# Reciprocal roots of the norms: a power operation on GpSimd in place of an integer guess and three Newton steps on VectorE

## The chip, the cores and the metric

The kernel runs on one core of a Trainium2 chip. The core has a matrix engine (TensorE, PE in the profile), a vector engine (VectorE, DVE), a scalar engine (ScalarE, ACT), a general engine (GpSimd, POOL) and a queue engine (SyncE, SP) that here only issues DMA transfers. Each engine works through its own list of instructions in order and waits on semaphores for results of the others. The metric is the device time of one execution in microseconds (us).

## The reference

One layer of an encoder over 1024 rows of 1024 features, in float32. Three blocks are added to the running rows, and a last norm closes the layer:

```python
x = x + 0.5 * swiglu_half_step(x, ffn1_norm, ffn1_w_in, ffn1_w_out)
x = x + hybrid_mixer(x, ...)      # attention heads and recurrent heads side by side
x = x + 0.5 * swiglu_half_step(x, ffn2_norm, ffn2_w_in, ffn2_w_out)
x = rms_norm(x, final_norm)

def rms_norm(x, gain):
    return x * lax.rsqrt(jnp.mean(x * x, axis=-1, keepdims=True) + 1e-6) * gain
```

The norm appears in many places: before each of the three blocks and at the end over a row of 1024 features, for each attention query and key head and each recurrent output head over 128 features, and over the 512 features of the attention output. In each of them the sum of squares of a row is turned into one factor, the reciprocal root of (sum / width + 1e-6). How that factor is computed is all that the change touches.

## The kernel before

Rows are handled in eight tiles of 128 rows, one row per partition, so a norm of a tile needs one factor per partition. `rstd(ss, n, width, tag)` (line 72) gets n sums of squares per partition and gives n factors. It is called 43 times:

- `pair1` (line 1224) normalizes the eight input tiles in pairs: the first two tiles by a call each with n = 1, the other three pairs by one call each with n = 2. ScalarE squares and sums the tile (line 1236), and one VectorE operation multiplies by factor and gain (line 1240).
- `row_rstd` and `norm_rows` (lines 118 and 129) do the same for the eight tiles ahead of the mixer (`done1`, names `n1`), the eight ahead of the second feed-forward block (`to_ffn`, names `n2`) and the eight of the output (`done2`, names `fin`), each with n = 1. The multiplication is line 132; where a row is worked in two halves, line 126 first adds the two sums.
- `head_norm` (line 825) has n = 8: four calls for the recurrent heads (`rec`), four for queries (`aq`), two for keys (`ak`). It squares on ScalarE, sums on VectorE (line 831), multiplies by the factor on VectorE (line 833) and by the gain on GpSimd (line 836).
- `attn_scale` (line 1064) has n = 2 and is called four times (`ao`): a matmul with a column of ones sums the squares, and the factor enters where the projection's result leaves PSUM (line 1079).

Inside, `rstd` works on VectorE alone. Line 83 scales the sums and adds the small constant, lines 84 and 85 make a first guess with integer operations on the bits of the number, and three Newton steps follow. A step is two operations when n = 1 (lines 89 and 95) and three otherwise (lines 93, 94, 95). So a call has 9 VectorE operations when n = 1 and 12 otherwise, each on at most 128 x 8 numbers and each needing the one before it.

The matmuls are arranged in stages. In `ffn_up` the normalized tiles are transposed on TensorE (line 183), split into two parts (lines 191 and 192; the difference on VectorE or GpSimd), and multiplied with weights that are loaded by SyncE's queue (line 255) and split in the same way (lines 104 and 105). `plain` (line 285) has the first matmuls (line 295), `product` the later ones (line 311); sums of blocks for a Strassen scheme are formed on VectorE (lines 237 to 240) and GpSimd (lines 272 to 275). `ffn_down` (line 443) multiplies with the second weight (line 515), adds to the rows (lines 542 and 581), and calls `done` for a finished tile. After the first feed-forward block, `follow1` transposes the normalized tile (line 148) for the mixer, whose first matmuls are line 168. In `mixer_in` the recurrent heads run with raised priority and projections fill in between; `attention` softmaxes (GpSimd multiplies half of the probabilities, line 985), projects (line 1032) and sends the rows to the second block through DRAM (lines 1085 and 1091, issued from GpSimd's queue).

The order of instructions on each engine isn't written by hand. The program is laid out by a planner (`schedule_with_timeline_sim=True`, line 1374) that plays the instructions through on estimated durations and, at each moment, gives a free engine the ready instruction of the highest priority; the source order and the marked high-priority stretches set the priorities. The result is a fixed list per engine. Tiles of one pool tag share a few buffers, so a load into a buffer also waits until the last reader of its earlier content is done; the input tiles and the raw weights of `ffn_up` share seven buffers.

Of the kernel before, what the change touches and what calls it, by code (L numbers as in the profile page):

```python
# [12 lines left out]
F32 = mybir.dt.float32  # L13
F32R = mybir.dt.float32r
I32 = mybir.dt.int32
U8 = mybir.dt.uint8
AF = mybir.ActivationFunctionType
ALU = mybir.AluOpType
# [3 lines left out]
P = 128  # L22
# [10 lines left out]
NREC = 4  # L33
NCH = T // P
EPS = 1e-6
RS_SCALE = 2.0 ** -28
RS_MAGIC = 0x5F3759DF - (1 << 23) - (1 << 31)
WHOLE = (slice(0, D),)
HALVES = (slice(0, D // 2), slice(D // 2, D))
LEVELS = (1, 2, 4, 8, 16, 32, 64)  # L40
# [5 lines left out]
class Trunk:  # L46
    def __init__(self, ctx, tc, io):
        self.tc, self.nc, self.io = tc, tc.nc, io
        nc = self.nc
        pool = lambda name, **kw: ctx.enter_context(tc.tile_pool(name=name, **kw))  # L50
        self.const = pool("const", bufs=1)
        self.gpool = pool("gains", bufs=1)
        self.stat = pool("stat", bufs=4)
        self.dpool = pool("scratch", bufs=1, space=bass.MemoryType.DRAM)
        self.ident = self.const.tile([P, P], F32, name="ident")
        pool("align", bufs=1, side="right").tile([P, 40], F32, name="align")
        make_identity(nc, self.ident)
        self.banks = {}

    def open_psum(self, ctx, prefix, **spec):  # L60
# [11 lines left out]
    def rstd(self, ss, n, width, tag):  # L72

        nc = self.nc
        work = self.stat.tile([P, 9, n], F32, name=f"rs_{tag}", tag=f"rs{n}")  # L80
        parts = iter(work[:, i, :] for i in range(9))
        v, t, w = next(parts), next(parts).bitcast(I32), next(parts)
        nc.vector.tensor_scalar(v, ss, RS_SCALE / width, RS_SCALE * EPS, ALU.mult, ALU.add)
        nc.vector.tensor_single_scalar(t, v.bitcast(I32), 1, op=ALU.logical_shift_right)
        nc.vector.tensor_scalar(w.bitcast(I32), t, -1, RS_MAGIC, ALU.mult, ALU.add)
        for c in (0.75, 3.0 * 2.0 ** -4, 3.0 * 2.0 ** -10):
            q, y = next(parts), next(parts)
            if n == 1:
                nc.vector.scalar_tensor_tensor(
                    out=q, in0=w, scalar=v, in1=w, op0=ALU.mult, op1=ALU.mult  # L90
                )
            else:
                nc.vector.tensor_mul(q, w, w)
                nc.vector.tensor_mul(q, q, v)
            nc.vector.scalar_tensor_tensor(
                out=y, in0=q, scalar=-c, in1=w, op0=ALU.add, op1=ALU.mult
            )
            w = y
        return w

    def split(self, hl, src, lo_engine=None):
# [1276 lines left out]
```

## Time and profile before

| | |
|---|---|
| median of 3 runs | 2008.72 us (2003.79 to 2009.0) |
| profiled execution, its own time | 2008.14 us |
| span of its instructions | 2006.0 us |
| mean granted TensorE clock | 0.991 |
| TensorE matmul busy | 1944.5 us (97%) |
| TensorE weight load busy | 1665.6 us (83%) |
| VectorE busy | 1329.7 us (66%), 1941 instructions |
| ScalarE busy | 807.4 us (40%) |
| GpSimd busy | 727.2 us (36%), 543 instructions |

A share is an average over the whole span. The time outside the span is start and end of the execution, 2.1 us here. In rows of groups, a line starts with the source line, engine, operation and operands by the program's names, then a count, busy time, mean duration of one, and the idle time of the engine ahead of it with what ended it. In rows of the timeline, the first number is the start and the second the duration, in us; brackets hold the idle time before. In rows of the chain of waits, the numbers are start and length of a piece.

### The profile page before, as it was taken

To read this page: it belongs to the slowest core of one execution; us is meant where nothing else is said; L and a number is where in the kernel's file an instruction comes from. 1 tells how busy PE (TensorE), PEld (TensorE's weight loads), DVE (VectorE), ACT (ScalarE), POOL (GpSimd) and SP (SyncE) were. 2 spreads that over 40 slices of the span, in tenths; PEclk is the share of its full clock that TensorE was granted. 3 is DMA by queue.
4 is the path that set the end of the run, shared out by engine and by line. 5 is a ranking of instruction groups with operands and counts; after the bars stand their busy time and mean duration, and the time that the engine had idled before them with its cause. 6 is when DMAs were issued, how large, how long until landed. Compare 5 with 4: busy or idle time off the path is not lost.

```text
span 2006.0 us, 26914 instructions
## 1 busy us (share of the span) xinstructions
PE 1944.5 (97%) x10157; PEld 1665.6 (83%) x10157; DVE 1329.7 (66%) x1941; ACT 807.4 (40%) x1269; POOL 727.2 (36%) x543
## 2 busy tenths in 40 slices
PE   5999999999899999999999999989999999999998
PEld 4888888888688789899899888878888888887886
DVE  8776676655865864588882558766556666566867
ACT  5433333334434432233332646644333333343433
POOL 2745555443660000021210333315555465435800
PEclk9999999999999999999999999989999999999999
DMA  6432333227844411121324443155433333259544
GB/s 206 142 117 78 116 120 96 79 100 278 303 147 131 152 32 39 47 74 33 105 64 156 138 161 113 64 210 167 138 100 105 105 100 95 77 186 331 184 121 158
DMA packets 219594, 259.34 MB, mean 129 GB/s; under 512 B 12596, under 2 KB 150088, under 8 KB 219464
## 3 DMA queue, kind: packets, MB, share of 16 engines
q1 hardware_dynamic: 210120, 226.15, 35.1%
q0 software_dynamic: 9344, 31.46, 4.0%
q8 instruction: 80, 1.31, 0.3%
q14 instruction: 50, 0.41, 0.1%
HBM read 185.21 MB, written 72.35 MB: 128 GB/s over the span
## 4 chain that ended last, share of the span: by engine, by line
PE 85%; DMA 6%; DVE 4%; ACT 2%; issue 1%; POOL 1%; SPq 0%; DVEq 0%; ACTq 0%; POOLq 0%
PE pa_ffn L311 16%; PE pd_ffn L311 11%; PE rec_ps L168 6%; PE pya_ffn L515 6%; PE pc_ffn L311 6%; PE pb_ffn L311 5%; PE pye_ffn L515 3%; PE pyd_ffn L515 3%; PE pyc_ffn L515 3%; PE lv L738 2%; PE pa L1032 2%; PE pp_ffn L295 2%; PE ri_ps L649 2%; PE aq_ps L649 2%; PE rg_ps L649 2%; PE py L1032 2%
## 5 line engine op out<-in xcount | busy, mean ns | idle before, releaser
L105 DVE TENSOR_TENSOR hl_in_ffn_A<-raw_in_ffn,hl_in_ffn_A 128x512 fp32r<-128x512 f32 x135 | 200.4, 1489 | 98.6 <-ACT hl_in_ffn_A L104 98.6
L311 PE MATMUL pa_ffn<-ffn_T,hl_in_ffn_S 128*128 128x512 f32 x984 | 242.7, 389 | 0.0
L311 PE MATMUL pd_ffn<-ffn_B,hl_in_ffn_S 128*128 128x512 f32 x960 | 232.7, 389 | 0.0
L311 PEld LDWEIGHTS pa_ffn<-ffn_T,hl_in_ffn_S 128*128 128x128 f32 x984 | 184.7, 188 | 38.4
L311 PEld LDWEIGHTS pd_ffn<-ffn_B,hl_in_ffn_S 128*128 128x128 f32 x960 | 180.2, 188 | 37.4
L105 DVE TENSOR_TENSOR hl_in_ffn_S<-s_ffn,hl_in_ffn_S 128x512 fp32r<-128x512 f32 x164 | 148.0, 907 | 64.1 <-ACT hl_in_ffn_S L104 63.7
L104 ACT CAST hl_in_ffn_S<-s_ffn 128x512 fp32r<-128x512 f32 x164 | 101.6, 622 | 220.2 <-PE pd_ffn L311 167.9
L104 ACT CAST hl_in_ffn_A<-raw_in_ffn 128x512 fp32r<-128x512 f32 x135 | 83.5, 625 | 155.0 <-PE pc_ffn L311 75.0
L105 DVE TENSOR_TENSOR hl_out_ffn_S<-raw_out_ffn_S,hl_out_ffn_S 128x512 fp32r<-128x512 f32 (+1 forms) x88 | 102.8, 1173 | 50.5 <-ACT hl_out_ffn_S L104 50.4
L105 DVE TENSOR_TENSOR hl_out_ffn_A<-raw_out_ffn_A,hl_out_ffn_A 128x1024 fp32r<-128x1024 f32 (+1 forms) x66 | 92.8, 1416 | 55.5 <-ACT hl_out_ffn_A L104 55.0
L273 POOL TENSOR_TENSOR s_ffn<-s_ffn,raw_in_ffn 128x512 f32<-128x512 f32 x41 | 65.7, 1602 | 172.1 <-issue 115.9
L515 PE MATMUL pya_ffn<-hl_out_ffn_S 128*128 128x512 f32 x528 | 122.8, 393 | 4.2 <-DVE hl_out_ffn_S L105 4.2
L168 PE MATMUL rec_ps<-hm,hl_rec_w 128*128 128x512 f32 x528 | 121.6, 390 | 1.9 <-DVE hm L152 1.9
L515 PEld LDWEIGHTS pya_ffn<-hl_out_ffn_S 128*128 128x128 f32 x528 | 100.0, 190 | 26.3 <-DVE hl_out_ffn_S L105 5.5
L311 PE MATMUL pb_ffn<-ffn_B,hl_in_ffn_A 128*128 128x512 f32 x492 | 119.8, 389 | 0.0
L311 PE MATMUL pc_ffn<-ffn_T,hl_in_ffn_A 128*128 128x512 f32 x492 | 118.8, 389 | 0.3 <-DVE hl_in_ffn_A L105 0.3
L311 PE MATMUL pa_ffn<-ffn_B,hl_in_ffn_A 128*128 128x512 f32 x492 | 119.0, 389 | 0.0
L104 ACT CAST hl_out_ffn_S<-raw_out_ffn_S 128x512 fp32r<-128x512 f32 (+1 forms) x88 | 73.5, 837 | 108.4 <-PE pya_ffn L515 41.1
L168 PEld LDWEIGHTS rec_ps<-hm,hl_rec_w 128*128 128x128 f32 x528 | 98.5, 188 | 22.3 <-DVE hm L152 2.2
L311 PEld LDWEIGHTS pc_ffn<-ffn_T,hl_in_ffn_A 128*128 128x128 f32 x492 | 92.3, 188 | 19.8 <-DVE hl_in_ffn_A L105 0.7
L311 PEld LDWEIGHTS pb_ffn<-ffn_B,hl_in_ffn_A 128*128 128x128 f32 x492 | 92.3, 188 | 19.2
L311 PEld LDWEIGHTS pa_ffn<-ffn_B,hl_in_ffn_A 128*128 128x128 f32 x492 | 92.3, 188 | 19.2
(291 smaller groups left out, 3969.3 us busy)
## 6 DMA issues: line engine op xcount, KB each, us to landing
raw_in_ffn<-in_ffn_w_in SPq DMA_DIRECT2D x88, 512.0 KB, 4.2
raw_out_ffn_S<-d_comb SPq DMA_DIRECT2D x88, 256.0 KB, 2.7
d_comb<-g_ffn POOLq DMA_DIRECT2D x82, 256.0 KB, 2.3
raw_out_ffn_A<-d_act SPq DMA_DIRECT2D x66, 256.0 KB, 5.4
ffn_kept<-in_ffn_w_out SPq DMA_DIRECT2D x65, 256.0 KB, 5.6
d_act<-g_ffn SPq DMA_DIRECT2D x62, 256.0 KB, 2.3
raw_out_ffn_A<-in_ffn_w_out SPq DMA_DIRECT2D x52, 256.0 KB, 4.1
x<-d_x SPq DMA_DIRECT2D x24, 512.0 KB, 5.5
```

Source lines behind the costliest of these rows:

```text
L104: nc.scalar.copy(hl[:, 0, :], src)
L105: (lo_engine or nc.vector).tensor_sub(hl[:, 1, :], src, hl[:, 0, :].bitcast(F32))
L168: nc.tensor.matmul(out, hl[:, a, ks], h[half][b][:, k, cols], start=(k == 0 and i == 0), stop=(k == NK - 1 and i == 2),)
L273: nc.gpsimd.tensor_sub(s2, s1, a11)
L295: nc.tensor.matmul(halves(ps[j]), A[2 * j + k // 4][:, a, ks], B[k // 4][:, :, b, k % 4, lo:hi], start=(k == 0 and i == 0), stop=(k == NK ...
L311: nc.tensor.matmul(ps, A[:, a, ks], op(key)[:, b, k, :], start=(first and k == 0 and i == 0), stop=(k == 3 and i == 2), skip_group_check=True,
L515: nc.tensor.matmul(ps, hl[:, a, j * P : (j + 1) * P], hl[:, b, hi], start=(first and i == 0 and n == 0), stop=(i == last and n == 2), skip ...
L649: nc.tensor.matmul(ps[:, tt, :], h[half][a][:, k, ts], hl[k // 4][:, b, ws], start=(k == 0 and i == 0), stop=(k == NK - 1 and i == 2),)
L738: nc.tensor.matmul(pl[:, cs], now[:, 0, cs], now[:, 1, cs], start=True, stop=True)
L1032: nc.tensor.matmul(py, lhs(a, n), units[n][:, b, ds], start=(n == 0 and i == 0), stop=(n == 3 and i == 2),)
```

## The change

Every call of `rstd` now has two operations. VectorE scales the sums and adds the constant (as before, without the extra scale that the integer guess needed), and GpSimd raises the result to the power of -0.5, with the exponent read from a small constant tile that is filled once at the start. The scratch of a call shrinks from nine rows to two.

```diff
+        self.neg_half = self.const.tile([P, NCH], F32, name="neg_half")
+        nc.vector.memset(self.neg_half, -0.5)
...
-        work = self.stat.tile([P, 9, n], F32, name=f"rs_{tag}", tag=f"rs{n}")
-        parts = iter(work[:, i, :] for i in range(9))
-        v, t, w = next(parts), next(parts).bitcast(I32), next(parts)
-        nc.vector.tensor_scalar(v, ss, RS_SCALE / width, RS_SCALE * EPS, ALU.mult, ALU.add)
-        nc.vector.tensor_single_scalar(t, v.bitcast(I32), 1, op=ALU.logical_shift_right)
-        nc.vector.tensor_scalar(w.bitcast(I32), t, -1, RS_MAGIC, ALU.mult, ALU.add)
-        for c in (0.75, 3.0 * 2.0 ** -4, 3.0 * 2.0 ** -10):
-            q, y = next(parts), next(parts)
-            if n == 1:
-                nc.vector.scalar_tensor_tensor(
-                    out=q, in0=w, scalar=v, in1=w, op0=ALU.mult, op1=ALU.mult
-                )
-            else:
-                nc.vector.tensor_mul(q, w, w)
-                nc.vector.tensor_mul(q, q, v)
-            nc.vector.scalar_tensor_tensor(
-                out=y, in0=q, scalar=-c, in1=w, op0=ALU.add, op1=ALU.mult
-            )
-            w = y
+        work = self.stat.tile([P, 2, n], F32, name=f"rs_{tag}", tag=f"rs{n}")
+        v, w = work[:, 0, :], work[:, 1, :]
+        nc.vector.tensor_scalar(v, ss, 1.0 / width, EPS, ALU.mult, ALU.add)
+        nc.gpsimd.tensor_tensor(out=w, in0=v, in1=self.neg_half[:, :n], op=ALU.pow)
         return w
```

More of the change, by code (lines that the diff above doesn't have):

```diff
@@ L35 @@
 EPS = 1e-6
-RS_SCALE = 2.0 ** -28
-RS_MAGIC = 0x5F3759DF - (1 << 23) - (1 << 31)
 WHOLE = (slice(0, D),)
```

## The prediction

> **What bounds the kernel now.** I read the page's first part, then busy time by stretch, then what TensorE waited for.
>
> ```profile
> span 2006.0 us, 26914 instructions
> ...
> PE 1944.5 (97%) x10157; PEld 1665.6 (83%) x10157; DVE 1329.7 (66%) x1941; ACT 807.4 (40%) x1269; POOL 727.2 (36%) x543
> ```
>
> ```profile
> 0.00:62.00 62.00, 39.64 (x207) 34.57 (x208) 47.09 (x107) 35.80 (x63) 18.57 (x19) 0.92 0.64 203
> ...
> 672.00:710.00 38.00, 33.23 (x165) 26.58 (x164) 26.47 (x83) 15.67 (x37) 0.00 (x0) 1.00 0.23 84
> 710.00:1056.00 346.00, 346.00 (x2489) 325.70 (x2488) 248.17 (x414) 113.23 (x129) 48.52 (x19) 1.00 0.19 58
> ...
> 1135.00:1335.00 200.00, 192.99 (x1157) 168.64 (x1155) 133.98 (x279) 106.72 (x195) 64.11 (x54) 1.00 0.38 130
> ...
> 1968.00:2006.00 38.00, 29.10 (x129) 23.77 (x127) 30.96 (x103) 12.95 (x28) 0.00 (x0) 0.92 0.37 140
> ```
>
> Columns are the stretch, its length, busy time of PE, weight load, DVE, ACT and POOL, then granted clock, DMA share and GB/s. TensorE is the bound: it lacks 2006.0 - 1944.5 = 61.5 us. So 395 fewer VectorE operations (26 calls go from 9 to 1, 17 from 12 to 1) are worth nothing as a sum. They are worth something only where TensorE stands still and a factor is late. Of its idle time 22.4 us lie in the first 62 us, 4.8 us at the change from the first feed-forward block to the mixer, 7.0 us in the attention and 8.9 us at the end. In the mixer it has none.
>
> ```profile
> PE pt_ffn_B L183 <- DVE rs_n L95: 9.1, 1, 9.1
> ...
> PE pa L1032 <- DVE x L1079: 3.2, 1, 3.2
> ...
> PE pt_n L148 <- DVE xn_n L132: 2.1, 2, 1.5
> ```
>
> These waits of TensorE end with a factor or with the multiplication that uses it: 9.1 us at the start, 3.2 us for the last attention scale, 2.1 us ahead of the mixer.
>
> **Price of one call, before.** The last output tile (timeline) shows a call with n = 1 that nothing interrupts, and what stands ahead of it:
>
> ```profile
> 1997.14 0.69 DVE L581 SCALAR_TENSOR_TENSOR x<-pye_ffn,x 128x512 f32<-128x512 f32 x1 [0.50 <-PE pye_ffn L515]
> ...
> 1997.86 0.63 ACT L122 ACTIVATE junk<-x 128x512 f32<-128x512 f32 x1 [4.03 <-DVE x L581]
> 1997.93 1.42 DVE L132 SCALAR_TENSOR_TENSOR x<-x,rs_fin,g_final 128x512 f32<-128x512 f32 x2
> 1998.40 0.19 ACT L122 ACTIVATION_READ_ACCUMULATOR junk<-x 128x1 f32 x1
> 1999.26 0.15 DVE L126 TENSOR_TENSOR ss_fin<-ss_fin 128x1 f32<-128x1 f32 x1
> 1999.45 0.15 DVE L83 TENSOR_SCALAR rs_fin<-ss_fin 128x1 f32<-128x1 f32 x1
> ...
> 2001.37 1.41 DVE L132 SCALAR_TENSOR_TENSOR x<-x,rs_fin,g_final 128x512 f32<-128x512 f32 x2
> ```
>
> From line 83 to the multiplication it is 2001.37 - 1999.45 = 1.92 us. For n = 2 the last attention scale gives 1334.81 - 1332.45 = 2.36 us (pieces of the chain, with starts):
>
> ```profile
> 1332.45 0.17 DVE rs_ao L83
> ...
> 1334.62 0.17 DVE rs_ao L95
> 1334.81 0.76 DVE x L1079
> ```
>
> **Price of one call, after.** Line 83 stays at 0.15 us. Then come a step to GpSimd, the power, and a step back. No row has a power. The nearest are GpSimd's other operations with two inputs, and the step from VectorE to it:
>
> ```profile
> L1023 POOL TENSOR_TENSOR ssq<-ssq,sq 128x256 f32<-128x256 f32 x9 | 7.2, 797 | 20.8 <-ACT sq L1022 20.7
> ...
> L871 POOL TENSOR_TENSOR aq<-aq,rope_aq 128x1024 f32<-128x1024 f32 x4 | 9.5, 2386 | 6.0 <-ACT aq L865 6.0
> ...
> L723 POOL TENSOR_TENSOR kd<-hx 128x1024 f32<-128x1024 f32 x4 | 12.8, 3188 | 154.5 <-ACT hx L716 122.6 <-issue 31.8
> ```
>
> ```profile
> 1043.58 1.22 DVE L833 TENSOR_TENSOR ak<-ak_ps,rs_ak 128x1024 f32<-128x1024 f32 x1
> ```
>
> ```profile
> 1044.95 2.35 POOL L836 TENSOR_TENSOR ak<-ak,g_attn_k_norm 128x1024 f32<-128x1024 f32 x1 [11.40 <-DVE ak L833]
> ```
>
> The step is 1044.95 - 1044.80 = 0.15 us; for the way back I take 0.05 us. From 256 to 1024 elements GpSimd pays (2386 - 797) / 768 = 2.07 ns per element, which leaves 797 - 530 = 0.27 us for one element. That is the lower end, as if a power cost no more than a product. The upper end is the longest row of all, 3.19 us. I take 0.5 us, between the intercept and the smallest whole operation seen (0.80), because one element per partition is nearest to the intercept and a power must cost more than a product. A call then takes 0.15 + 0.15 + 0.5 + 0.05 = 0.85 us, against 1.92 and 2.36. It breaks even where the power takes 1.92 - 0.35 = 1.57 us. The one memset at the start lies in VectorE's idle 4.7 us ahead of the first call and costs nothing.
>
> **The end: 1.7 us.** The last line 581 ends at 1997.83, and ScalarE's sum at 1998.59. Line 126 then starts at 1999.26 only because the previous tile's line 132 (1997.93, 1.42 us) stands before it, late through its own Newton steps. With a short call that multiplication is over before 1997.14. So line 126 starts at 1998.62, line 83 at 1998.81, the power runs from 1999.11 to 1999.61, and line 132 starts at 1999.66 instead of 2001.37. GpSimd is empty in this stretch (0.00, x0).
>
> **The last attention scale: 1.5 us.** 2.36 - 0.87 (line 83 takes 0.17 here). TensorE's 3.2 us of waiting ahead of the last projection covers it.
>
> **The change to the mixer: 2.0 us.** Timeline:
>
> ```profile
> 682.14 0.15 DVE L126 TENSOR_TENSOR ss_n<-ss_n 128x1 f32<-128x1 f32 x1
> ...
> 687.14 1.41 DVE L132 SCALAR_TENSOR_TENSOR xn_n<-x,rs_n,g_mix_norm 128x512 f32<-128x512 f32 x2
> 688.00 0.42 PEld L148 LDWEIGHTS pt_n<-ident,xn_n 128*128 128x128 f32 x4 [1.93 <-issue]
> ```
>
> Here one call takes 5.0 us from line 126 to line 132, since other operations stand between its nine, and one of them (line 581) waits for TensorE's last product. With two operations the multiplication can run by about 683.2, and the transposes fall inside TensorE's earlier matmuls. TensorE lacks 4.8 us in this stretch; the part that ends with this multiplication is the 2.1 us above, and that is the most I count. The least is nothing, if the multiplication stays behind line 581. I take 2.0, near the top, because GpSimd is empty here.
>
> **The start: 4.4 us.** Timeline, then chain:
>
> ```profile
> 5.56 0.15 DVE L83 TENSOR_SCALAR rs_n<-ss_n 128x1 f32<-128x1 f32 x1 [4.71 <-ACT junk L1236]
> ...
> 7.69 1.28 DVE L1240 SCALAR_TENSOR_TENSOR x<-x,rs_n,g_ffn_norm 128x1024 f32<-128x1024 f32 x1
> ...
> 12.25 0.62 ACT L104 CAST hl_in_ffn_A<-raw_in_ffn 128x512 fp32r<-128x512 f32 x1
> ...
> 13.18 1.28 DVE L1240 SCALAR_TENSOR_TENSOR x<-x,rs_n,g_ffn_norm 128x1024 f32<-128x1024 f32 x1
> ...
> 14.37 0.69 DVE L105 TENSOR_TENSOR hl_in_ffn_A<-raw_in_ffn,hl_in_ffn_A 128x512 fp32r<-128x512 f32 x1
> ...
> 17.30 8.99 PE L295 MATMUL pp_ffn<-ffn_B,hl_in_ffn_A 128*128 128x256 f32 x48 [0.81 <-ACT ffn_B L191]
> ```
>
> ```profile
> by line: DMA raw_in_ffn<-in_ffn_w_in 13.9%; DVE ffn_B L192 13.0%; DVE x L1240 12.3%; issue 11.1%; DMA x<-in_x 9.7%; DMA d_t_ffn<-t_ffn 8.8%; POOL ffn_T L192 7.9%; DVE rs_n L95 3.0%; ACT ffn_T L191 2.7%; DVE rs_n L93 2.4%; DVE t_ffn L238 2.1
> ...
> 15.09 6.04 DMA x<-in_x
> ...
> 39.11 1.17 DVE rs_n L95
> ```
>
> The first multiplication moves from 7.69 to 6.4. The second, whose nine steps were strewn among splits, moves from 13.18 to about 8.5. Next late is the fourth weight half: its cast ends at 12.87, so line 105 runs at 12.9 to 13.6 instead of 14.37 to 15.06. The load of an input tile that waits for its buffer then moves up from 15.09 by 1.5 us (lower end), and the first matmuls by up to 17.3 - 13.6 = 3.7 us. Behind that the chain spends 3.0% + 2.4% of some 62 us, 3.3 us, in Newton steps; all of it regained gives 7.0 us (upper end). I take 4.4, the middle being 4.3.
>
> One of these steps took 1.17 us where others take 0.15, while GpSimd was subtracting:
>
> ```profile
> 35.83 4.43 POOL L192 TENSOR_TENSOR ffn_T<-t_ffn,ffn_T 128x512 fp32r<-128x512 f32 x2 [5.53 <-ACT ffn_T L191]
> ```
>
> The Trainium skill (SBUF — State Buffer, Who interferes with whom) says that a VectorE instruction with two SBUF inputs and a GpSimd instruction that reads SBUF block each other for a whole instruction. By that rule, with which this row agrees, such a stall passes to the next VectorE operation instead of vanishing; about 2 us of the 3.3 would then stay, the middle would be 3.3 us, and the sum 1.1 us smaller.
>
> **What costs nothing.** In the mixer ten calls with n = 8 gain or lose nothing: TensorE is busy 346.00 of 346.00 us there. The power waits for line 83 in GpSimd's list, and lines 836, 871 and 723 queue behind it; or it queues behind them. If that cover were gone, ten calls could each be late by one line 723 and the power less the old twelve steps, 3.19 + 0.87 - 2.36 (twelve operations, as in the attention scale) = 1.7 us, 17 us in all. In the attention line 985 and the issues at lines 1085 and 1091 stand behind a waiting power; the call shrinks by about as much as one line 985 could delay it, so I count nothing for the first three scales and the norms behind them.
>
> **Sum.** 1.7 + 1.5 + 2.0 + 4.4 = 9.6 us. From the profiled 2008.14 us that gives 1998.5 us; the runs' median is 0.6 us above the profiled execution. With the unknown costs at their friendly ends (a power of 0.27 us in four calls on the path, 0.9 us; the mixer's change at 2.1; the start at 7.0) it is 1994.9; with the start at 1.5 and the mixer's change at nothing it is 2003.4.
>
> **The rivals.** One: the loads set the start and line 581 still stands in the way ahead of the mixer. For it: the chain holds 13.9% raw weight loads. Against it: the second multiplication waits for its factor, not for a load. Time: 2008.14 - 1.7 - 1.5 - 1.5 = 2003.4.
>
> Two, the slower side: the power is long. For it: GpSimd pays 2.07 ns per element even for a product, where line 1240 on VectorE pays 1.28 us / 1024 = 1.25 ns; against it: a call has one number per partition. It decides from 1.57 us. At 3.19 us a call with n = 1 loses 1.6 us: two in a row at the start, two ahead of the mixer, one at the end, and 1.2 us at the attention scale: 9.2 us, 2017.3.
>
> Three: only the first power is long, as its code has to come in. No row shows such a thing, as every two-input GpSimd row is a product, sum or difference. Priced like the load of an input tile (6.04 us, above), the first call takes 6.4 us where it took 7.69 - 5.56 = 2.13, so the start loses 4.3 us: 2008.14 - 5.2 + 4.3 = 2007.2. The Trainium skill (GPSIMD Engine Reference, Instruction dispatch) says that the first call of a freshly loaded GpSimd kernel pays about 6 us with no instruction in the profile; no run here shows it.
>
> Four: the planner lays the lists out anew and the queue on GpSimd costs the mixer its cover. For it: GpSimd's list in the mixer has operations of 2.4 to 3.2 us. Against it: TensorE has no idle time there. At the full price it is 1998.5 + 17 = 2015.5.
>
> **How the numbers follow.** Forecast 0.57, rival one 0.20, two 0.09, three 0.06, four 0.08. About 0.3%, 6 us, is what a measurement of this kernel can tell from no change: below 2002.7 counts as faster, above 2014.7 as slower. The forecast lies below but for a small part (0.53 faster); rivals one and three are in between, as is most of four, whose price is rarely paid in full; two is slower, with the rest of four (0.12). The range runs from 1994 to 2010, which leaves out two and half of four above and a little below; the forecast's own is 1994.9 to 2003.
>
> **What would show it.** Right: a GpSimd power of about 0.5 us; line 132 of the last tile within 0.9 us of its line 83; the wait ahead of line 183 down from 9.1 to about 7.8 us; the first line 295 at 13 to 15 us; waits for line 1079 under 2 us; 346 us of busy TensorE in the mixer. Wrong: a power over 1.57 us, new waits of TensorE on GpSimd, or a start of the matmuls that stays at 17.

## The result and the profile after

The changed kernel takes 2027.61 us (median of four runs, 2026.74 to 2028.35), beside 2006.55 us for the kernel before: a ratio of 1.0101, with an interval of 1.0087 to 1.0115. It is slower by 1%. The forecast was 1998.5 us. The profiled execution took 2027.26 us, its span 2025.3 us, against 2008.14 and 2006.0 us before.

In the changed file every line behind `rstd` has a number lower by 15: 311 is now 296, 515 is 500, 132 is 117. The power is line 83, the operation before it line 82. Here is the page's first part for the changed kernel.

```profile
span 2025.3 us, 26561 instructions
...
PE 1968.2 (97%) x10157; PEld 1665.1 (82%) x10157; DVE 1231.4 (61%) x1547; ACT 806.2 (40%) x1269; POOL 763.7 (38%) x586
```

VectorE has lost 394 operations and 98 us of work, as planned. TensorE runs the same 10157 matmuls, but is busy for 23.7 us longer (1968.2 against 1944.5), while its idle time fell from 61.5 to 57.1 us. So the time was not lost in waits. The groups of instructions of TensorE, kept apart by shape, show where (count, then busy us and mean ns of one); first before, then after:

```profile
L311 PE MATMUL pa_ffn<-ffn_T,hl_in_ffn_S 128*128 128x512 f32 x984 | 242.7, 389 | 0.0
L311 PE MATMUL pd_ffn<-ffn_B,hl_in_ffn_S 128*128 128x512 f32 x960 | 232.7, 389 | 0.0
```

```profile
L296 PE MATMUL pa_ffn<-ffn_T,hl_in_ffn_S 128*128 128x512 f32 x984 | 248.9, 396 | 0.0
L296 PE MATMUL pd_ffn<-ffn_B,hl_in_ffn_S 128*128 128x512 f32 x960 | 237.8, 395 | 0.0
```

The up products of both feed-forward blocks are slower, each one, with the same operands and shapes, and they wait for nothing. Busy time by stretch gives the step from one matmul to the next. The columns are the stretch, its length, busy time with counts of PE, weight load, DVE, ACT, POOL, then granted clock, DMA share and GB/s. The two stretches are the up products of the first and of the second block, before and after:

```profile
62.00:463.00 401.00, 400.75 (x1768) 331.24 (x1767) 262.84 (x280) 147.29 (x254) 206.86 (x166) 1.00 0.32 101
1403.00:1784.00 381.00, 381.00 (x1682) 315.49 (x1681) 221.47 (x253) 135.70 (x235) 187.98 (x156) 1.00 0.32 102
```

```profile
57.00:470.00 413.00, 412.88 (x1770) 331.91 (x1769) 229.78 (x279) 148.04 (x255) 203.81 (x168) 1.00 0.31 99
1414.00:1806.00 392.00, 392.00 (x1682) 315.58 (x1681) 209.31 (x252) 134.54 (x233) 185.26 (x154) 1.00 0.30 97
```

TensorE is full in both, at clock 1.00 in both, and in the second stretch the count is the same 1682 matmuls: 381.00 / 1682 = 226.5 ns before, 392.00 / 1682 = 233.1 ns after. The matmul costs 6.6 ns more.

To see all stages I took from both traces the start of the first or last matmul of each tile name. These are the lengths between such marks, in us:

| stretch | before | after | difference |
|---|---|---|---|
| start to first up product (line 311 / 296) | 62.43 | 57.17 | -5.26 |
| up products, first block | 400.55 | 412.13 | +11.58 |
| down products, first block | 222.90 | 222.65 | -0.25 |
| last down product to first `rec_ps` | 20.94 | 18.29 | -2.65 |
| mixer, to first `s` of the attention | 395.45 | 394.65 | -0.80 |
| attention, to last `pv` | 224.77 | 229.13 | +4.36 |
| last `pv` to first product of the second block | 22.05 | 19.70 | -2.35 |
| from there to its first up product | 53.66 | 59.74 | +6.08 |
| up products, second block | 380.57 | 391.77 | +11.20 |
| down products, second block | 212.93 | 211.71 | -1.22 |
| last down product to the end | 9.32 | 7.94 | -1.38 |

The sum of the differences is +19.3 us, the difference of the spans. The gains that were forecast are there, 11.6 us at the four places. Against them stand 22.8 us in the up products, for which the prediction had no term, and 10.4 us at two places that it counted as nothing.

The power itself is as cheap as was taken. Groups of line 83 on GpSimd, then the last output tile in the timeline:

```profile
L83 POOL TENSOR_TENSOR rs_n<-rs_n,neg_half 128x1 f32<-128x1 f32 x18 | 11.1, 618 | 95.1 <-DVE rs_n L82 91.9 <-DVE ss_n L111 3.3
L83 POOL TENSOR_TENSOR rs_ao<-rs_ao,neg_half 128x2 f32<-128x2 f32 x4 | 2.9, 726 | 21.3 <-DVE rs_ao L82 21.3
L83 POOL TENSOR_TENSOR rs_aq<-rs_aq,neg_half 128x8 f32<-128x8 f32 x4 | 6.6, 1643 | 82.0 <-DVE rs_aq L82 82.0
L83 POOL TENSOR_TENSOR rs_fin<-rs_fin,neg_half 128x1 f32<-128x1 f32 x8 | 7.6, 953 | 77.6 <-DVE rs_fin L82 77.6
```

```profile
2017.83 0.69 DVE L566 SCALAR_TENSOR_TENSOR x<-pye_ffn,x 128x512 f32<-128x512 f32 x1 [0.79 <-PE pye_ffn L500]
...
2019.50 0.15 DVE L82 TENSOR_SCALAR rs_fin<-ss_fin 128x1 f32<-128x1 f32 x1
2019.79 0.55 POOL L83 TENSOR_TENSOR rs_fin<-rs_fin,neg_half 128x1 f32<-128x1 f32 x1 [4.20 <-DVE rs_fin L82]
2020.38 1.41 DVE L117 SCALAR_TENSOR_TENSOR x<-x,rs_fin,g_final 128x512 f32<-128x512 f32 x2 [0.73 <-POOL rs_fin L83]
```

From line 82 to the multiplication it is 2020.38 - 2019.50 = 0.88 us, where it was 1.92. The step to GpSimd is 0.14 us, the power 0.55, the way back 0.04.

### The profile page after: what moved, and what is told of

It is laid out like the page before. It is cut to its first block, busy times and chain, and to the rows that moved or that the text cites. A ratio compares the mean times of both kernels' runs of the same rounds, so it can differ in the third digit from the quotient of the medians.

```text
span 2025.3 us, 26561 instructions
## 1 busy us (share of the span) xinstructions
PE 1968.2 (97%) x10157; PEld 1665.1 (82%) x10157; DVE 1231.4 (61%) x1547; ACT 806.2 (40%) x1269; POOL 763.7 (38%) x586
## 4 chain that ended last, share of the span: by engine, by line
PE 84%; DMA 7%; DVE 4%; issue 2%; ACT 2%; POOL 1%; SPq 0%; DVEq 0%; POOLq 0%; ACTq 0%
PE pa_ffn L296 17%; PE pd_ffn L296 11%; PE rec_ps L153 6%; PE pya_ffn L500 6%; PE pc_ffn L296 6%; PE pb_ffn L296 6%; PE pye_ffn L500 3%; PE pyd_ffn L500 3%; PE pyc_ffn L500 3%; PE lv L723 2%; PE pp_ffn L280 2%; PE ri_ps L634 2%; PE aq_ps L634 2%; PE rg_ps L634 2%; PE pa L1017 2%
## 5 line engine op out<-in xcount | busy, mean ns | idle before, releaser
L296 PE MATMUL pa_ffn<-ffn_T,hl_in_ffn_S 128*128 128x512 f32 x984 | 248.9, 396 | 0.0
L296 PE MATMUL pd_ffn<-ffn_B,hl_in_ffn_S 128*128 128x512 f32 x960 | 237.8, 395 | 0.0
L90 DVE TENSOR_TENSOR hl_in_ffn_A<-raw_in_ffn,hl_in_ffn_A 128x512 fp32r<-128x512 f32 x135 | 160.3, 1194 | 102.1 <-ACT hl_in_ffn_A L89 102.1
L90 DVE TENSOR_TENSOR hl_out_ffn_A<-raw_out_ffn_A,hl_out_ffn_A 128x1024 fp32r<-128x1024 f32 (+1 forms) x66 | 98.5, 1501 | 49.8 <-ACT hl_out_ffn_A L89 49.0
L296 PE MATMUL pa_ffn<-ffn_B,hl_in_ffn_A 128*128 128x512 f32 x492 | 123.4, 396 | 0.0
L296 PEld LDWEIGHTS pc_ffn<-ffn_T,hl_in_ffn_A 128*128 128x128 f32 x492 | 92.4, 188 | 22.8 <-ACT hl_in_ffn_A L89 0.6
```

The source lines that it names most:

```text
L90: (lo_engine or nc.vector).tensor_sub(hl[:, 1, :], src, hl[:, 0, :].bitcast(F32))
L296: nc.tensor.matmul(ps, A[:, a, ks], op(key)[:, b, k, :], start=(first and k == 0 and i == 0), stop=(k == 3 and i == 2), skip_group_check=True,
```

## Where a matmul of the same shape gets slower: operands apart in SBUF

The diff adds a tile of 32 bytes per partition (`neg_half`) to a pool at the left end of SBUF and shrinks the scratch of `rstd` from 2560 to 1280 bytes. Pools are laid one behind the other from both ends. So every buffer of the left side behind these moves by +32 - 1280 = -1248 bytes; those of the right side stay. In the up products the stationary operand is a weight tile `hl_in_ffn` (pool `wop`, left), the moving operand a tile `ffn_B` or `ffn_T` (right). By the allocation of the built programs the first `wop` buffer stood at 42816 before and stands at 41568 after; `ffn_B` is at 163648 and `ffn_T` at 114496 in both. Modulo 256 all three were 64; after, the weights are at 96. The kernel before holds a tile `align` at the right end that nothing reads; it sets just this.

Theory: the slower step comes from where the two operands stand to each other. Rivals: it comes from the work on GpSimd or the new lists, or from where one of the operands stands by itself. Seven kernels tell these apart. Each diff is against the kernel named.

`a_pad32`, after, left side moved by 32 bytes more (the weights are then alike with the moving operand modulo 64):

```diff
-        self.gpool = pool("gains", bufs=1)
+        pool("pad", bufs=1).tile([P, 8], F32, name="pad"); self.gpool = pool("gains", bufs=1)
```

> The changed kernel with one unused tile of 32 bytes per partition after the constants, so that all buffers on the left side of SBUF start at a multiple of 64 bytes again, as before the change; every engine's list of instructions is the one of the changed kernel. Theory A (placement: the 32-byte exponent tile moved the buffers by half of 64 bytes and made each matmul of line 296 about 7 ns slower, 233 instead of 227 ns from start to start): 226.7 ns per matmul, mean 389 instead of 396 ns, time about 2027.6 - 3450 x 0.0067 = 2004 us or a little under. Theory B (the new order of the lists, or the power operations themselves, make the matmuls slower): stays within 3 us of 2027.6.

Measured: 2029.66 us, ratio 1.0119 (1.0098 to 1.0141). My expectation was wrong: alike modulo 64 isn't enough.

`b_left32`, before, with nothing of the change but shifted buffers: the left side by 32 bytes (the same line), the right side by 64:

```diff
-        pool("align", bufs=1, side="right").tile([P, 40], F32, name="align")
+        pool("align", bufs=1, side="right").tile([P, 24], F32, name="align")
```

> The kernel before with an unused tile of 32 bytes ahead of the left-side buffers (weights' halves of the first product at 32 modulo 64) and the right side moved by 64 bytes (the h operands stay at a multiple of 64); lists of instructions unchanged. Theory A: slow, 2006.6 + 23 = about 2030 us, L311 at 233 ns from start to start. Theory B: no change, 2006.6 within 3 us.

Measured: 2030.88 us, ratio 1.0124 (1.0106 to 1.0142).

`b_right32`, before, only the right side moved by 32 bytes (`[P, 32]` for `[P, 40]`):

> The kernel before with the right side alone moved by 32 bytes: moving operands of line 311 at 32 modulo 64, weights at 0. Theory A1 (the two operands of a matmul must lie alike modulo 64): slow, about 2030 us. Theory A2 (only where the weights start counts): as before, 2006.6 within 3 us, except where weights lie on the right side (line 168, 816 + 48 matmuls of 512 columns, up to 5 us more). Theory B: no change.

Measured: 2030.98 us, ratio 1.0125 (1.0104 to 1.0146).

`b_both32`, before, both sides moved by 32 bytes:

> The kernel before with both sides moved by 32 bytes, so that all operands lie at 32 modulo 64. Theory A1 (alike modulo 64): as before, 2006.6 within 3 us, L311 at 227 ns. Theory A2 (where the weights start): slow, at least 2030 us, and the matmuls of line 515, whose operands share one tile, slower too (2650 of them, up to 18 us more). Theory B: no change.

Measured: 2006.01 us, ratio 0.9994 (0.9981 to 1.0007).

For the last two the rows of the groups of TensorE follow, first `b_right32`, then `b_both32`:

```profile
L311 PE MATMUL pa_ffn<-ffn_T,hl_in_ffn_S 128*128 128x512 f32 x984 | 249.2, 395 | 0.0
...
L168 PE MATMUL rec_ps<-hm,hl_rec_w 128*128 128x512 f32 x528 | 121.6, 390 | 1.9 <-DVE hm L152 1.9
...
L1032 PE MATMUL py<-hl_wor,recT 128*128 128x512 f32 x192 | 47.6, 397 | 0.0
```

```profile
L311 PE MATMUL pa_ffn<-ffn_T,hl_in_ffn_S 128*128 128x512 f32 x984 | 242.7, 389 | 0.0
...
L168 PE MATMUL rec_ps<-hm,hl_rec_w 128*128 128x512 f32 x528 | 121.6, 390 | 1.9 <-DVE hm L152 1.9
...
L1032 PE MATMUL py<-hl_wor,recT 128*128 128x512 f32 x192 | 46.6, 392 | 0.0
```

With Newton steps and not one power, moving one side by 32 bytes makes the products as slow as in the changed kernel; moving the other side along makes them as fast as before. So it isn't the power, nor the lists, nor the place of one operand by itself: it is how the two sides stand to each other. Moving a side shifts every buffer on it, so the runs alone don't single out the two operands of a matmul; the other rows do. The matmuls of line 168 have both operands on the right side and stay at 390 ns, while those of `py` (line 1032, `hl_wor` on the right, `recT` on the left) go from 392 to 397 ns with the up products. Only matmuls whose operands lie on different sides get slower.

How far apart counts the same? Two more pads on the changed kernel, and one kernel that has the exponent in the unused `align` tile:

`a_pad96` (`[P, 24]`; the weights then differ by 128 modulo 256):

> The changed kernel with an unused tile of 96 bytes: the weights' halves lie like the h operands modulo 128 (both 64), but 128 bytes apart modulo 256. Lists of instructions are those of the changed kernel. If alike modulo 128 is enough: fast, line 296 at 389 ns mean, about 2002 us (before 2005.3 less the 4 to 5 us that TensorE stands still less). If 256 or more is needed: slow, about 2028 us.

Measured: 2025.87 us, ratio 1.0087 (1.0064 to 1.0111): slow.

`a_pad1248` (`[P, 312]`; the large buffers stand where the kernel before has them):

> The changed kernel with an unused tile of 1248 bytes: every large buffer at the address that it has before the change, lists of instructions those of the changed kernel. Theory A (placement is the whole loss): line 296 at 389 ns mean, about 2002 us, 3 to 5 us faster than before, most of it at the start (first line-296 matmul near 57 us instead of 62). Theory B (order or power cost something besides): above 2006 us.

Measured: 2003.11 us, ratio 0.9983 (0.9971 to 0.9996).

`a_align`, after, the left side moved by -1280 bytes against before, a multiple of 256 but not of 512:

```diff
-        pool("align", bufs=1, side="right").tile([P, 40], F32, name="align")
+        self.neg_half = pool("align", bufs=1, side="right").tile([P, 40], F32, name="align")
         make_identity(nc, self.ident)
-        self.neg_half = self.const.tile([P, NCH], F32, name="neg_half")
-        nc.vector.memset(self.neg_half, -0.5)
+        nc.vector.memset(self.neg_half[:, :NCH], -0.5)
```

> The changed kernel with its exponent in the so far unused tile at the right end of SBUF instead of a new constant, so that no buffer moves for it; the smaller scratch of a call still moves the left side by 1280 bytes, which is a multiple of 256 but not of 512. If alike modulo 128 or 256 is enough: fast, about 2002 us. If 512 or more is needed: slow, about 2028 us.

Measured: 2002.44 us, ratio 0.9971 (0.9958 to 0.9984). Its stretches of up products, with the list of instructions unchanged:

```profile
58.00:458.00 400.00, 400.00 (x1766) 330.95 (x1765) 236.79 (x278) 147.31 (x253) 201.82 (x166) 1.00 0.31 102
1400.00:1780.00 380.00, 380.00 (x1678) 314.67 (x1677) 218.79 (x251) 135.00 (x234) 185.71 (x154) 1.00 0.31 100
```

400.00 / 1766 = 226.5 ns again. Alike modulo 256 is fast (distance 0 and 1280 from before); 32, 64 and 128 apart is slow, each by about the same. Within every kernel the operands of these matmuls already lie at many multiples of 512 bytes from each other, so a distance that counts only modulo 256 fits all runs; distances between 128 and 256 bytes weren't tried. Against the changed kernel `a_align` takes 25 us less in the profiled span (2000.4 against 2025.3) by moving buffers alone. This is the main cause, and it is shown by taking it away and by making it in the kernel before.

The Trainium skill (SBUF — State Buffer, Who interferes with whom) gives TensorE two independent read ports, one for the moving operand and one for weight loads, and names the port pair of VectorE and GpSimd as the only place of contention. The measurements differ: with no other operation changed, the distance of the two operands moved the step from 226.5 to 233 ns. That the two reads meet somewhere is the likely reading, but no run shows where; the runs only show that distance decides.

## What the power is worth where it is used

With the placement put right the net gain was 3 to 6 us (ratios 0.9983, 0.9971), not the 10 that the four places promise. The next kernels keep all large buffers where the kernel before has them and choose call by call between power and Newton steps:

```diff
+    def by_power(self, tag, n):
+        return tag.startswith("n0_")
...
+        if self.by_power(tag, n):
+            nc.vector.tensor_scalar(v, ss, 1.0 / width, EPS, ALU.mult, ALU.add)
+            nc.gpsimd.tensor_tensor(out=w, in0=v, in1=self.neg_half[:, :n], op=ALU.pow)
+            return w
```

`c_start`: power only in the five calls of the input tiles (`n0_`).

> The kernel before with the power in the five calls of the input tiles alone, exponent in the unused right-end tile, all addresses as before. If the start's gain (5.3 us earlier first matmul of the product in the changed kernel's trace) is kept to the end: about 2000 us, at least as fast as the full change at these addresses. If it is lost again at the next place bound by loads (464 to 532 us): 2005 us, no change.

Measured: 1999.76 us, ratio 0.9961 (0.9945 to 0.9977). The start takes 56.61 us instead of 62.43; the stretches behind it are as before, but for up to 1.2 us.

`c_best`: power in the input tiles, at the change to the mixer and in the output (`n0_`, `n1_`, `fin`), which are 21 calls, 18 with n = 1 and three with n = 2 (the count in the expectation is wrong).

> All large buffers stand where the kernel before has them; the power is used in the calls of the first feed-forward block's start, of the change to the mixer and of the output tiles (25 calls of n = 1 and the pair of two), the Newton steps stay in the mixer, the attention and the calls ahead of the second feed-forward block. Theory (the call's own gain comes where TensorE waits for a factor, and the losses of 6.1 us at the start of the second block and of 2 to 5 us in the attention belong to the lists that the other calls get): start -5.0 us, change to the mixer -2.6, tail -1.4, nothing else moves: 9.0 us less than before, 1997.5 us, ratio 0.9955. Rival (the losses come with any power on GpSimd, by its queue): the start of the second block is near 59.7 us again instead of 53.7 and the time near 2003.5, ratio 0.9985.

Measured: 1996.11 us, ratio 0.9941 (0.9924 to 0.9958), the lowest of all and clear of both kernels, though the interval overlaps that of `c_start`. Start 57.84, change to the mixer 18.30, tail 7.64 us, and the attention (225.03) and the start of the second block (52.83) stay as they were. The theory's gains came at their places: -4.6, -2.6 and -1.7 us. A further 2.6 us came between the last `pv` and the second block, where this kernel still has Newton steps. That is TensorE's clock, as the stretches of the last projection show, first before (with the two parts around the moment the clock fell), then `c_best` (with TensorE's wait):

```profile
1332.20:1343.60 11.40, 8.19 (x26) 6.46 (x27) 6.99 (x25) 1.66 (x3) 1.08 (x2) 0.70 0.55 200
...
1331.00:1334.40 3.40, 1.41 (x9) 1.16 (x7) 1.63 (x10) 0.00 (x0) 0.00 (x0) 1.00 1.02 397
1334.40:1341.20 6.80, 5.58 (x13) 4.42 (x14) 4.67 (x15) 1.66 (x3) 0.82 (x2) 0.50 0.39 132
```

```profile
1324.30:1333.20 8.90, 5.69 (x27) 4.66 (x27) 6.62 (x25) 1.66 (x3) 0.63 (x2) 1.00 0.55 199
...
PE pa L1040 <- DVE x L1087: 3.2, 1, 3.2
```

TensorE waits for the scale for 3.2 us in both. After that wait the granted clock (third number from the end) is 0.70 in the one execution and 1.00 in the other, and the same matmuls take 8.19 or 5.69 us. The Trainium skill (TensorE: Matmul & The Clock Gate, Part 1: The HAM clock gate) says that the clock falls after an idle window of about 3.4 us, and that the windows run freely, so that by this rule it matters where in a window a wait falls. The rows agree in that equal waits of 3.2 us left the clock at 0.50 in one execution and at 1.00 in the other. They differ in that the window needn't be idle: in the 3.4 us ahead of the fall TensorE was busy for 1.41 us. So of each difference of 1 to 3 us behind such a wait, a part may be chance and not the change.

`c_ffn2`: power only in the eight calls ahead of the second block (`n2_`).

> All large buffers stand where the kernel before has them; the power is used only in the calls ahead of the second feed-forward block. Theory (these calls' new place in the lists puts a cast of a weight half ahead of the cast that TensorE needs): the stretch from the block's first product with the input tile to its first up product grows from 53.7 to about 59.7 us, the time by 6 us less what the attention gains at its end: ratio 1.002 to 1.003. Rival (the loss belongs to the attention scale and the calls of n = 8): the stretch stays at 53.7 us, ratio 0.999 to 1.000.

Measured: 2011.36 us, ratio 1.0022 (1.0008 to 1.0037). The total is as the theory has it, but for another reason: the stretch at the start of the second block stays at 53.68 us, as the rival has it, and the attention grows from 224.77 to 229.35 us.

`c_mix`: power only in the calls with n = 8 and n = 2 (`rec`, `aq`, `ak`, `ao`).

> All large buffers stand where the kernel before has them; the power is used only in the calls of n = 8 and in the attention scales (n = 2). Theory: the attention loses 2 to 5 us up to its last product with the values and gains 2.3 us behind it, the start of the second block stays at 53.7 us: ratio 0.9995 to 1.0015. Rival (the loss at the start of the second block comes from these calls): that stretch is near 59.7 us and the ratio near 1.003.

Measured: 2008.24 us, ratio 1.0008 (0.9994 to 1.0022). The attention takes 227.19 us, the way from there to the second block 19.68 instead of 22.05, the start of that block 53.70. Gain and loss cancel.

So in the attention the power has a price in either kind of call. The waits of TensorE there, first before, then the changed kernel (engine, line, what it waited for: us, times, longest):

```profile
PE s L975 <- ACT p L982: 5.0, 2, 3.7
PE ptp L994 <- DVE pT L998: 1.1, 2, 0.5
```

```profile
PE ptp L979 <- DVE pT L983: 4.5, 5, 1.5
PE s L960 <- ACT p L967: 3.9, 2, 3.6
```

The transposes now wait for VectorE five times instead of twice, 3.4 us more, on an operation (line 983) that has nothing to do with a factor. The split of the probabilities comes later in VectorE's new list. These two readings locate a part of the loss; which power moved which operation wasn't tried. Two other parts are not the lists. With one list order the stretch took 227.07 us in `a_align` at a clock of 1.00 and 228.73 us in `c_all` at 0.99, so about 1.7 us can be the clock. And placement alone, with the old lists, made it 225.89 us in `b_right32` against 224.77 before, which is 1.1 us.

## One cast at the start of the second block

The 6.1 us at the start of the second block appeared in the changed kernel, in `a_align` and in `a_pad1248`, but neither in `c_ffn2` nor in `c_mix`. ScalarE's timeline of `a_align` shows what stands in the way, and TensorE's waits in that stretch name the casted tile:

```profile
1350.38 0.38 ACT L285 ACTIVATE sg_ffn<-pp_ffn 128x256 f32<-128x256 f32 x1
1353.82 0.62 ACT L88 CAST hl_in_ffn_A<-raw_in_ffn 128x512 fp32r<-128x512 f32 x1 [3.05 <-DMA raw_in_ffn<-in_ffn_w_in]
1354.34 1.07 ACT L175 CAST ffn_B<-pt_ffn_B 128x512 fp32r<-128x512 f32 x2
```

```profile
PE pp_ffn L279 <- ACT ffn_B L175: 7.9, 2, 4.3
```

ScalarE stands still for 3 us for a weight load that nobody needs yet, and behind it in its list stand the casts of the transposed tile for which TensorE waits. Lists are fixed, so the second can't pass the first. When all calls but one (tile 1 of `n2_`) use the power, the planner puts this one cast behind the two others; apart from it two more casts of ScalarE's list move by a few places. The subtractions that belong to these casts move along on VectorE, and in the attention some operations of VectorE and TensorE change places too, so this isn't a change of one position alone.

`c_but1`, that kernel:

```diff
+    def by_power(self, tag, n):
+        return not tag.startswith("n2_1")
```

> All calls by the power as in the changed kernel, large buffers where the kernel before has them, except that one call of the 43, the norm of tile 1 ahead of the second feed-forward block, keeps its Newton steps. In ScalarE's list ahead of the up products of the second block this moves one operation: the cast of a weight half that waits for its load stands behind the two casts of the transposed tile (line ffn_B) instead of ahead of them. Theory (this one position is what costs the start of the second block its time): the stretch from its first product with the input tile to its first up product is 53.5 to 55.5 us instead of 59.8, and the time about 1997, ratio 0.995. Rival (the power itself, or the load, sets that stretch): it stays at 59 to 60 us, time near 2002, ratio 0.9975.

Measured: 2001.94 us, ratio 0.9972 (0.9961 to 0.9982). The stretch fell to 54.65 us as the theory has it, and the total stayed where the rival has it. So it was measured again side by side with `c_all`, in which all 43 calls use the power and the buffers stand as before.

> All 43 calls by the power, all buffers where the kernel before has them; measured side by side with the kernel that leaves one call to Newton steps. Theory (the place of one cast in ScalarE's list costs about 5 us of the total): stretch at the start of the second block 59.7 us, ratio about 0.9975 to 0.9985, and 0.0025 above its neighbour. Rival (the stretch is longer, but the total gets it back elsewhere, or other stretches scatter by as much): both ratios within 0.001 of each other.

> The same kernel as before with one call of the 43 by Newton steps, measured side by side with the one that has all by the power. Theory: stretch at the start of the second block 54.7 us, ratio about 0.995, 0.0025 below its neighbour. Rival: ratio within 0.001 of its neighbour, near 0.997 to 0.998.

Measured: `c_all` 2002.22 us, ratio 0.9981 (0.9972 to 0.9989); `c_but1b` 2001.40 us, ratio 0.9979 (0.9969 to 0.9988). The stretch took 59.73 us in the one trace and 53.91 in the other. In `c_but1b` the two casts stand ahead of the load again, and its wait for the load holds up nothing that TensorE needs:

```profile
1354.19 1.08 ACT L199 CAST ffn_B<-pt_ffn_B 128x512 fp32r<-128x512 f32 x2
1357.37 0.62 ACT L112 CAST hl_in_ffn_A<-raw_in_ffn 128x512 fp32r<-128x512 f32 x1 [2.10 <-DMA raw_in_ffn<-in_ffn_w_in]
```

In the traces the stretch is 5 to 6 us longer with the cast in front, in four traces against two. In the total the two kernels differ by 0.8 us, less than their intervals resolve, and the ratios lie within 0.001 of each other, as the rival has it. The spans of these two traces differ by 3.0 us (2001.3 and 1998.3), but the one execution was 0.95 us slower than the median of its kernel and the other 0.9 us faster. The clock takes part in the stretch itself: between the two traces TensorE stands still for 5.2 us instead of 1.0 (59.80 - 54.61 and 53.90 - 52.85), and is busy for 1.8 us longer, at 0.91 against 0.95. First `c_all`, then `c_but1b`:

```profile
1341.00:1400.80 59.80, 54.61 (x289) 47.90 (x290) 33.25 (x48) 26.80 (x48) 28.36 (x21) 0.91 0.57 175
```

```profile
1343.70:1397.60 53.90, 52.85 (x288) 46.38 (x289) 35.04 (x48) 26.65 (x49) 27.85 (x21) 0.95 0.63 195
```

One giver-back is visible, the clock again: with the same lists in the last projection, TensorE was busy there for 5.55 us at clock 1.00 in `c_all` and for 7.15 us at 0.81 in `c_but1b`.

```profile
1327.90:1335.30 7.40, 5.55 (x25) 4.56 (x26) 3.67 (x6) 1.66 (x3) 2.45 (x4) 1.00 0.63 219
```

```profile
1329.00:1338.00 9.00, 7.15 (x26) 5.66 (x26) 3.76 (x6) 1.66 (x3) 2.45 (x4) 0.81 0.65 234
```

That is 1.6 us. Where the rest goes in the executions that weren't profiled can't be seen; why the total doesn't gain what the stretch does stays open.

## Why the prediction was wrong

**What failed: no term for where the buffers stand.** The prediction read the diff as instructions removed and added. "The one memset at the start ... costs nothing" is all that it says of the new tile, and the smaller scratch has no sentence. The sum needed a term of 3450 matmuls (1768 + 1682) by 6.6 ns, which is 22.8 us; this is what turned -3.4 us (`a_pad1248`: ratio 0.9983) into +20.3 (1.0101). The rows of before couldn't give the 6.6 ns, since nothing in them was slow, but the unread `align` tile next to the changed line was a sign that placement matters here. None of the rivals had it either.

**Price of a call: right.** 0.55 us for the power where 0.5 was taken, 0.88 us for the call where it was 0.85. Rival two falls: the mean power of one number is 0.62 us, and 0.95 in the output tiles, and the longest took 1.52, all below the break-even of 1.57. The long ones coincide with work on VectorE. Four of the eight powers of the output tiles took 1.20 to 1.52 us, and each ran while VectorE was in an operation with two inputs from SBUF; the other four ran with VectorE still and took 0.55 us. The last long one:

```profile
1998.53 3.67 DVE L117 SCALAR_TENSOR_TENSOR x<-x,rs_fin,g_final 128x1024 f32<-128x1024 f32 x3
1998.70 1.52 POOL L83 TENSOR_TENSOR rs_fin<-rs_fin,neg_half 128x1 f32<-128x1 f32 x1 [0.94 <-DVE rs_fin L82]
```

Rival three falls too: the first power of all takes as long as the others. It is in the timeline of the start:

```profile
5.68 0.55 POOL L83 TENSOR_TENSOR rs_n<-rs_n,neg_half 128x1 f32<-128x1 f32 x1 [4.39 <-DVE rs_n L82]
...
7.20 0.55 POOL L83 TENSOR_TENSOR rs_n<-rs_n,neg_half 128x1 f32<-128x1 f32 x1 [0.96 <-DVE rs_n L82]
...
7.64 2.48 DVE L1225 SCALAR_TENSOR_TENSOR x<-x,rs_n,g_ffn_norm 128x1024 f32<-128x1024 f32 x2 [0.52 <-DMA g_ffn_norm<-in_ffn_norm]
...
13.29 0.79 PE L280 MATMUL pp_ffn<-ffn_B,hl_in_ffn_A 128*128 128x256 f32 x2 [0.64 <-ACT ffn_B L176]
```

**The start, 4.4 us: right in size, one step wrong.** 5.3 us came. The first matmuls start at 13.29 us instead of 17.30, inside the 13 to 15 named. But the first multiplication didn't move to 6.4: its factor is ready at 7.75 for the second tile and at 6.23 for the first, and it starts at 7.64, because the load of the gain row ends only then. So the wait ahead of the first transposes is 9.0 us, not 7.8 (first of the rows below). The gain is all from the second tile, whose steps no longer lie among the splits. The 3.3 us of the side sentence on the shared port were too little.

**The change to the mixer, 2.0 us: right.** The stretch gave 2.65. Waits of TensorE, changed kernel:

```profile
PE pt_ffn_B L168 <- DVE x L1225: 9.0, 1, 9.0
...
PE pa L1017 <- DVE x L1064: 1.8, 1, 1.8
...
PE pt_n L133 <- DVE xn_n L117: 0.7, 1, 0.7
```

The wait for `xn_n` fell from 2.1 to 0.7 us; where the rest of the 2.65 came from wasn't followed. Rival one, by which line 581 still stands in the way, falls.

**The last attention scale, 1.5 us: right.** The wait fell from 3.2 to 1.8 us. The stretch gave 2.35; the rest is the clock in the last projection, 0.81 where before it was 0.70:

```profile
1339.20:1348.20 9.00, 7.15 (x25) 5.68 (x25) 3.76 (x6) 1.66 (x3) 2.45 (x4) 0.81 0.64 231
```

**The end, 1.7 us: right.** From the end of the last line 566 (2018.52) to the multiplication it is now 1.86 us; before it was 2001.37 - 1997.83 = 3.54. That is 1.7 us at the multiplication; 1.4 arrived at the end of the span.

**The mixer at nothing: right.** Its stretch in the changed kernel:

```profile
710.00:1056.00 346.00, 345.53 (x2474) 324.74 (x2475) 232.06 (x309) 112.55 (x129) 65.19 (x29) 1.00 0.19 58
```

TensorE is busy for 345.53 of 346.00 us, and rival four's 17 us weren't there.

**The attention and the start of the second block at nothing: wrong.** In the traces they cost 4.4 and 6.1 us, the second with little to see in the total. The argument was on line 985 on GpSimd; the loss came mostly by the planner's new lists on VectorE and ScalarE, with the clock and the placement in it as said above. Rival four had the mechanism, new lists, at the wrong place. With the placement right (2003.11 us in `a_pad1248`, 2002.44 in `a_align`), the forecast of 1998.5 would have been some 4 us low.

## What to carry to other kernels

A diff that adds or resizes a tile also moves every tile allocated behind it, so ask of each hot matmul whether its two operands still stand as they did; keep new small tiles in space that is already there. Where the same instructions get slower with nothing to wait for, shift a buffer in the old kernel before looking for another cause. A cheaper operation pays where an engine stands still for it: with the power in 21 of the 43 calls the kernel was at its fastest, while in the other 22 the gain at the last attention scale was lost again by lists that came out worse.

## What the runs showed of the hardware

- A matmul with 512 columns of this kind took 226.5 ns from start to start when stationary and moving operand stood alike modulo 256 bytes, and 233 ns when they were 32, 64 or 128 bytes apart. Matmuls with both operands on one side of SBUF kept their time. Only one shape and data type was looked at closely.
- After a wait of TensorE of 3.2 us the granted clock over the next projection was 1.00 in one execution and 0.70 in another of nearly the same lists, 2.5 us of difference in 24 matmuls. The clock fell to 0.50 after 3.4 us in which TensorE was busy for 1.41 us.
- GpSimd's power of two tensors took 0.55 us for one number per partition when VectorE was still, 0.73 for two and 1.64 for eight. With one number the mean over the output tiles was 0.95 us: those that ran beside a VectorE operation with two inputs from SBUF took 1.20 to 1.52 us.
